# A gated delta rule on Trainium2: the triangular inverse of its chunks formed from 64x64 products in quarters of the PE array

## The chip, the core and the metric

One NeuronCore of a Trainium2 chip runs the whole program. Its engines work side by side and wait for each other by semaphores: TensorE (PE in the profile, its weight loads PEld), VectorE (DVE), ScalarE (ACT), GpSimd (POOL) and SyncE (SP), which issues most of the DMAs. The metric is the device time of one execution in microseconds (us), lower is better.

## What is computed

The reference is a trunk of two layers over 1024 tokens of width 1024. The first layer mixes tokens with a gated delta rule (4 heads) beside stick-breaking attention (8 heads), the second with multi-scale retention; a SwiGLU FFN follows each. The change touches only the delta rule:

```python
def gated_delta_rule(q, k, v, g, beta):            # GDN_CHUNK = 64
    ...
    g = lax.cumsum(g.reshape(b_, h, n, c), axis=3)
    dec_strict = jnp.exp(jnp.where(strict, gdiff, -jnp.inf))
    kb = k * beta[..., None]
    lower = jnp.einsum('bhnid,bhnjd->bhnij', kb, k) * dec_strict
    tri = jnp.eye(c, dtype=lower.dtype) + lower
    rhs = jnp.concatenate([v * beta[..., None], kb * jnp.exp(g)[..., None]], axis=-1)
    sol = lax.linalg.triangular_solve(tri, rhs, left_side=True, lower=True, unit_diagonal=True)
    ...
    def step(state, inp):
        u_n, w_n, a_n, q_n, k_n, gl_n = inp
        v_new = u_n - jnp.einsum('bhcd,bhde->bhce', w_n, state)
        o_n = jnp.einsum('bhcd,bhde->bhce', q_n, state) + jnp.einsum('bhij,bhje->bhie', a_n, v_new)
        state = state * jnp.exp(gl_n)[..., None, None] + jnp.einsum('bhcd,bhce->bhde', k_n, v_new)
        return state, o_n
```

Per head and chunk a unit lower triangular matrix is solved against a right-hand side. The kernel works in chunks of 128 tokens and forms the inverse of that matrix (transposed) outright.

## The kernel before

The program runs through stages: the adaLN modulation and the first norm, the hybrid projection with the delta rule woven into it, stick-breaking attention, the first layer's output and FFN, retention, and the second FFN. Nearly all of its time goes to matmuls of the projections, done in three passes on high and low parts (`mm3`, lines 159 to 161, 128x512 each, tiles named `gps`, `fps`, `ops`).

The change lies in the stage that the profile shows from about 100 to 602 us. There, the remaining projection work (generators `gemm_gen`, tile `gps`; `v_gen`, tile `vps`; the q/k norms, tile `qst`) is the filling between the steps of the delta rule. One step of filling is one k-slice of a projection tile, three 128x512 matmuls.

The delta rule is cut into 8 units, `g_unit(h, b)`, one for each head h and half b of the tokens. A unit handles four chunks of 128 tokens side by side: a tile of 128x512 holds four 128x128 matrices. It is a generator, and each `yield` ends a step. Its steps are: decays (`gd`, `egr`), the norms of k and q (`gst`), the transpose of v (`vT`), `kk` (the products of k with itself, from which DVE makes the upper triangular `U2`), `kT` and `qk`, then the inverse, then the recurrence over the four chunks (`seq`), and the output norm.

The inverse is built by block doubling. Masks (`gc[:, 2 + l]`) cut level l of U2 into `Ul` on POOL. Level 0 gives `Y = I - U0`. Each of the levels 1 to 6 then takes three steps: the PE transposes Y into `X`; the PE forms `W` from Ul and X; the PE forms `dY` from W and Y, and DVE subtracts it from Y. Between them X is copied out of PSUM by ACT or DVE in turn, and W by ACT:

```python
            for l in range(1, 7):
                for c in range(4): PE.transpose(cc(ps, c), cc(Y, c), ident)                      # L742
                (A.copy if l % 2 else V.tensor_copy)(X, ps)                                      # L745
                for c in range(4): PE.matmul(cc(ps, c), cc(u, c), cc(X, c), ...)                 # L749
                A.copy(W, ps)                                                                    # L752
                for c in range(4): PE.matmul(cc(ps, c), cc(W, c), cc(Y, c), ...)                 # L756
                V.tensor_tensor(Y, Y, ps, op=ALU.subtract)                                       # L758
```

An fp32 matmul leaves two records in the profile, a transpose one; a step of four 128x128 matmuls is a row of eight records, and a step of four transposes a row of four.

The order of the PE's instructions is written out by the program (`manual_schedule` over the PE alone); the other engines' order is made by the scheduler, in which the copies of the inverse have a raised priority. The loop at the end of the stage keeps up to three units alive; a new one starts when the youngest has gone `GSTAG` = 14 steps. Each round lets every live unit do one step, and after each step issues a number of filling steps: a credit made of `GFILL` (by how many units live), a weight `GW` for the kind of step, and the filling that is left over the steps that are left. `GSTEPS` says how many steps a unit is counted for.

Of the kernel before, what the change touches and what calls it, by code (L numbers as in the profile page):

```python
# [52 lines left out]
C_ID, C_ONE, C_STRICT, C_INCL, C_NSTR, C_NCOM, C_NEG, C_BLK, C_LEV = 0, 1, 2, 3, 4, 5, 6, 7, 8  # L53
# [8 lines left out]
def tile_trunk(ctx: ExitStack, tc: tile.TileContext, xT, cT, adaS, adaT, vec, w_ab, w_hyb, w_hout, w_rin, w_rout,  # L62
               w_fin, w_fout, cst, rcst, out):
    nc = tc.nc
    V, A, G, PE = nc.vector, nc.scalar, nc.gpsimd, nc.tensor
# [19 lines left out]
    ident, ones = cs[:, 0, :], cs[:, 1, :]  # L85
# [491 lines left out]
    with tc.manual_schedule(engines=PEONLY):  # L577
# [29 lines left out]
        for k in range(8):  # L607
# [22 lines left out]
    with ExitStack() as sx:  # L630
        gq = sx.enter_context(tc.tile_pool(name="gdn", bufs=2, side="right"))
        pb = sx.enter_context(tc.tile_pool(name="pb", bufs=4, space=PSUM))
        gc = gq.tile([P, 9, P], F32, tag="gc", name="gc", bufs=1)
        nc.sync.dma_start(gc[:, 0:2, :], cst[:, C_STRICT:C_INCL + 1, :])
        nc.sync.dma_start(gc[:, 2:9, :], cst[:, C_LEV:C_LEV + 7, :])
# [4 lines left out]
        def bc(ap):  # L640
            return ap.unsqueeze(1).broadcast_to([P, 4, P])
# [4 lines left out]
        r4 = lambda t: t.rearrange("p (c n) -> p c n", c=4)  # L646
        bank = lambda nm: pb.tile([P, HT], F32, tag="b", name=nm)
# [9 lines left out]
        def g_unit(h, b):  # L657
            sl = slice(b * HT, b * HT + HT)
            cs = slice(4 * b, 4 * b + 4)
            tl = lambda tag, bufs: gq.tile([P, HT], F32, tag=tag, name=f"{tag}{h}{b}", bufs=GB.get(tag, bufs))  # L660
            io = []
            for j in range(3):
                t = tl("kn", 3) if j == 1 else tl("gin", 4)
# [9 lines left out]
            ps = bank("gd")  # L673
# [7 lines left out]
            ps = bank("egr")  # L681
# [19 lines left out]
            cc = lambda t, c: t[:, c * P:c * P + P]  # L701
            ps = bank("vT")
# [9 lines left out]
            V.tensor_tensor(U2, ps, Eb, op=ALU.mult)  # L712
            ul = []

            def level(l):
                t = tl("Ul", 3)
                G.tensor_tensor(r4(t), r4(U2), bc(gc[:, 2 + l, :]), op=ALU.mult)
                return t
            u0, u1 = level(0), level(1)
            Y = tl("Y", 2)  # L720
            V.tensor_tensor(r4(Y), bc(ident), r4(u0), op=ALU.subtract)
            yield
            ps = bank("kT")
            for c in range(4):
# [4 lines left out]
            ps = bank("qk")  # L729
            for c in range(4):  # L730
                PE.matmul(cc(ps, c), cc(k, c), cc(q, c), start=(c == 0), stop=True, skip_group_check=True)
            AT = tl("AT", 3)
            V.tensor_tensor(AT, ps, Em, op=ALU.mult)
            yield
            un = u1
            for l in range(1, 7):
                u = un
                if l < 6:
                    un = level(l + 1)
                ps = bank("X")  # L740
                for c in range(4):
                    PE.transpose(cc(ps, c), cc(Y, c), ident)  # L742
                X = tl("X", 1)
                with tc.high_priority(offset=3000):
                    (A.copy if l % 2 else V.tensor_copy)(X, ps)  # L745
                yield "X"
                ps = bank("W")
                for c in range(4):
                    PE.matmul(cc(ps, c), cc(u, c), cc(X, c), start=(c == 0), stop=True, skip_group_check=True)  # L749
                W = tl("W", 2)  # L750
                with tc.high_priority(offset=3000):
                    A.copy(W, ps)  # L752
                yield "W"
                ps = bank("dY")
                for c in range(4):
                    PE.matmul(cc(ps, c), cc(W, c), cc(Y, c), start=(c == 0), stop=True, skip_group_check=True)  # L756
                with tc.high_priority(offset=3000):
                    V.tensor_tensor(Y, Y, ps, op=ALU.subtract)  # L758
                yield "Y"
# [81 lines left out]
        with tc.manual_schedule(engines=PEONLY):  # L841
            gg_ = [gemm_gen(hs, g_evac(i)) for i in range(2, 16)]
            fills = gg_ + [v_gen(0, lambda: gst.tile([P, HT], F32, tag="gy", name="gyv", bufs=2))] + qk_gens
            fill(fills, 8)
            decays()
            heads = {h: gg_[max(4 * h - 2, 0):4 * h + 2] for h in range(4)}
            sizes = {id(g): 32 if i == 14 else 16 for i, g in enumerate(fills)}
            left = 8 * GSTEPS

            def ngroups():  # L850
                return sum(sizes[id(g)] for g in fills) - 8
            units = [(h, b) for h in range(4) for b in range(2)]
            live = []
            credit = 0.0
            acb = []
            aq = [(i, ch, dt) for i in range(2) for ch in (2, 4, 3, 5) for dt in range(8)]

            def ada_half():
                if not aq:
                    return  # L860
                i, ch, dt = aq.pop(0)
                if (ch, dt) == (2, 0):
                    acb.append(gq.tile([P, HT], F32, tag="acb", name="acb", bufs=1))
                    nc.sync.dma_start(acb[i], cb_d[:, i * HT:i * HT + HT])
                w = half_tile()
                j = ch * 8 + dt
                nc.sync.dma_start(w, adaT[j][:, i * HT:i * HT + HT])
                V.scalar_tensor_tensor(w, w, 1.0, acb[i], op0=ALU.mult, op1=ALU.mult,
                                       accum_out=(mod, mod2)[i][:, j:j + 1])
                if i and dt == 7:  # L870
                    ada_finish(0, ch)
            while units or live:
                while units and len(live) < 3 and (not live or live[-1][1] >= GSTAG):
                    h, b = units.pop(0)
                    while any(g in fills for g in heads[h]):
                        fill(fills, 1)
                    live.append([g_unit(h, b), 0])
                for u in list(live):
                    try:
                        hint = next(u[0])  # L880
                        u[1] += 1
                    except StopIteration:
                        live.remove(u)
                        continue
                    left -= 1
                    if left % 4 == 0:
                        ada_half()
                    credit += GFILL[len(live)] * GW.get(hint, 1.0) * ngroups() / max(left, 1)
                    fill(fills, int(credit))
                    credit -= int(credit)  # L890
                    if len(fills) <= SFIRST and not scrs:
                        s_first()
            fill(fills, 999)
            if not scrs:
                s_first()
            while aq:
                ada_half()
# [8 lines left out]
    with ExitStack() as sx:  # L906
# [99 lines left out]
        with tc.manual_schedule(engines=COMPUTE):  # L1006
# [17 lines left out]
            fills = [v_gen(1, stage3)]  # L1024
# [8 lines left out]
            for n in range(-6, 88):  # L1033
                p, m = n // 20, n % 20
# [25 lines left out]
                for tok in SORDER:  # L1060
# [6 lines left out]
                    else:  # L1067
                        i = n + int(tok[1:])
# [471 lines left out]
    o, fpa = ret["o"], ret["fpa"]  # L1540
# [362 lines left out]
```

## Time and profile before

| | |
|---|---|
| device time, median of 3 runs | 3121.37 us (3117.11 to 3124.62) |
| the profiled execution: its time, its span | 3122.01 us, 3120.1 us |
| the clock granted to TensorE, mean | 0.994 |
| PE, DVE, ACT, POOL busy, share of the span | 96%, 68%, 40%, 15% |
| the stage of the delta rule, first to last filling step | about 100 to 602 us |
| records of the inverse on the PE (L742, L749, L756) | 192, 384, 384 |

How to read it: a group row of the profile names the line, the engine, the operation, what it writes and reads, the shape and the count, then its busy time, the mean length of one in ns, and the idle time of its engine just ahead of it with what ended that. A timeline row begins with its start and its length in us; rows that follow each other in the same group are merged (x8). The PE is pipelined: a record lasts longer than the distance to the next one, so what an instruction costs the PE is read from start to start.

### The profile page before, as it was taken

The numbers are of one execution on the slowest core, as the hardware profiler recorded it, in microseconds if no ns is written. First come the engines' busy times: TensorE is split into PE (matmuls) and PEld (weight loads), VectorE is DVE, ScalarE is ACT, GpSimd is POOL, SyncE is SP. The second block draws the span as 40 slices with busy tenths as digits, with TensorE's granted clock in tenths as the row PEclk, the third lists the DMA queues.
The fourth block names the chain that finished last, engine by engine and source line by source line (L and its number), as shares of the span: only waits on it lengthen the run. The fifth ranks groups of instructions, "written<-read, shape, count | busy, mean of one in ns | idle before, by whom it ended". The sixth has DMA issues, their size and how long they took to land. (4 is left out here: it accounts for less than half of the span.)

```text
span 3120.1 us, 38627 instructions
## 1 busy us (share of the span) xinstructions
PE 3004.1 (96%) x14616; PEld 2415.6 (77%) x14616; DVE 2117.9 (68%) x3065; ACT 1244.7 (40%) x2011; POOL 461.7 (15%) x332
## 2 busy tenths in 40 slices
PE   7989999999989999999999999999999899999999
PEld 4778788867667888877878788887777688887887
DVE  6778976599887655588582455578866975556445
ACT  5445456688763222221263333333233632223111
POOL 0333332177440000000030000001111300000000
PEclk9999999999999999999999999999999999999999
DMA  5433332331034322287124333362312352225222
GB/s 215 135 102 122 116 111 73 105 132 45 28 112 149 105 81 81 100 307 260 61 92 152 116 118 111 108 234 92 109 48 70 123 155 85 81 81 167 91 74 101
DMA packets 136602, 362.35 MB, mean 116 GB/s; under 512 B 15072, under 2 KB 24032, under 8 KB 135904
## 3 DMA queue, kind: packets, MB, share of 16 engines
q1 hardware_dynamic: 135808, 358.90, 34.4%
q8 instruction: 115, 1.88, 0.2%
q10 hardware_dynamic: 464, 0.79, 0.1%
q14 instruction: 71, 0.58, 0.1%
q0 software_dynamic: 144, 0.20, 0.0%
HBM read 282.76 MB, written 77.07 MB: 115 GB/s over the span
## 5 line engine op out<-in xcount | busy, mean ns | idle before, releaser
L307 DVE SCALAR_TENSOR_TENSOR x<-ops,mod,x 128x512 f32<-128x512 f32 x288 | 215.3, 749 | 217.9 <-PE ops L161 217.4
L139 ACT CAST whi<-raw 128x1024 fp32r<-128x1024 f32 x158 | 165.5, 1051 | 401.2 <-PE ops L160 305.8
L159 PE MATMUL ops<-hdh,whi 128*128 128x512 f32 x704 | 277.3, 394 | 9.0 <-DVE x L307 8.5
L140 DVE TENSOR_TENSOR wlo<-raw,whi 128x1024 fp32r<-128x1024 f32 x158 | 208.2, 1319 | 104.6 <-ACT whi L139 99.8
L160 PE MATMUL ops<-hdl,whi 128*128 128x512 f32 x704 | 275.7, 392 | 0.0
L161 PE MATMUL ops<-hdh,wlo 128*128 128x512 f32 x704 | 275.5, 391 | 0.0
L159 PEld LDWEIGHTS ops<-hdh,whi 128*128 128x128 f32 x704 | 133.0, 189 | 43.9 <-DVE x L307 14.0
L159 PE MATMUL gps<-hh,whi 128*128 128x512 f32 x352 | 166.1, 472 | 0.0
L161 PEld LDWEIGHTS ops<-hdh,wlo 128*128 128x128 f32 x704 | 132.7, 189 | 28.4 <-issue 0.2
L160 PEld LDWEIGHTS ops<-hdl,whi 128*128 128x128 f32 x704 | 133.0, 189 | 27.3 <-issue 0.2
L195 POOL TENSOR_TENSOR nscr<-nscr 128x512 f32<-128x512 f32 x30 | 46.2, 1541 | 692.7 <-ACT nscr L194 635.0
L1269 ACT CAST thi<-raw 128x512 fp32r<-128x512 f32 x180 | 101.8, 618 | 112.0 <-DVE raw L1265 66.7
L160 PE MATMUL gps<-hl,whi 128*128 128x512 f32 x352 | 140.6, 400 | 0.0
L161 PE MATMUL gps<-hh,wlo 128*128 128x512 f32 x352 | 139.5, 396 | 0.0
L956 POOL TENSOR_TENSOR sl<-ab,sh 128x512 fp32r<-128x512 f32 (+1 forms) x80 | 116.2, 1453 | 140.7 <-ACT ab L940 73.8
L159 PE MATMUL ops<-osh,whi 128*128 128x512 f32 x320 | 127.1, 402 | 10.1 <-DVE x L307 8.1
L160 PE MATMUL ops<-osl,whi 128*128 128x512 f32 x320 | 126.6, 397 | 5.0 <-DVE osl L1757 4.5
L161 PE MATMUL ops<-osh,wlo 128*128 128x512 f32 x320 | 125.0, 392 | 0.0
L1270 DVE TENSOR_TENSOR tlo<-raw,thi 128x512 fp32r<-128x512 f32 x180 | 119.2, 709 | 3.3 <-ACT thi L1269 3.3
L1408 ACT ACTIVATE u<-u 128x512 f32<-128x512 f32 x44 | 27.8, 633 | 231.5 <-DVE u L1339 231.5
L1339 DVE TENSOR_TENSOR u<-u,mE 128x512 f32<-128x512 f32 x60 | 41.2, 687 | 112.5 <-PE mE L1279 112.5
L1319 DVE TENSOR_TENSOR u<-u,mB 128x512 f32<-128x512 f32 x60 | 41.2, 687 | 111.4 <-issue 100.1
(425 smaller groups left out, 8434.8 us busy)
## 6 DMA issues: line engine op xcount, KB each, us to landing
raw<-in_w_fin_dram SPq DMA_DIRECT2D x102, 512.0 KB, 3.8
raw<-in_w_rin_dram SPq DMA_DIRECT2D x64, 512.0 KB, 3.9
raw<-in_w_fout_dram SPq DMA_DIRECT2D x52, 512.0 KB, 3.6
adaw<-in_adaT_dram SPq DMA_DIRECT2D x48, 512.0 KB, 4.8
oraw<-hid_d SPq DMA_DIRECT2D x44, 512.0 KB, 6.1
gth<-in_adaT_dram SPq DMA_DIRECT2D x64, 256.0 KB, 3.0
raw<-in_w_hyb_dram SPq DMA_DIRECT2D x28, 512.0 KB, 3.7
hid_d<-c SPq DMA_DIRECT2D x44, 256.0 KB, 2.0
```

The source lines that it names most:

```text
L139: A.copy(hi, raw)
L140: V.tensor_tensor(lo, raw, hi.bitcast(F32), op=ALU.subtract)
L159: PE.matmul(ps, whi, xh, start=start, stop=False)
L160: PE.matmul(ps, whi, xl, start=False, stop=False)
L161: PE.matmul(ps, wlo, xh, start=False, stop=stop)
L195: (V if k > 5 else G).tensor_tensor(acc, acc, sq, op=ALU.add)
L307: V.scalar_tensor_tensor(xs[dt][:, sl], ps, gts(dt), xs[dt][:, sl], op0=ALU.mult, op1=ALU.add)
L956: G.tensor_tensor(s["sl"], s["ab"], s["sh"].bitcast(F32), op=ALU.subtract)
L1269: A.copy(hi, t)
L1270: e.tensor_tensor(lo, t, f32(hi), op=ALU.subtract)
L1319: V.tensor_tensor(s["u2"], s["u2"], s["S2"], op=ALU.add)
L1339: V.tensor_tensor(s["u3"], s["u3"], s["E"], op=ALU.add)
```

## The change

The four 128x128 matrices of a unit are each seen as 2x2 blocks of 64. Levels 0 to 5 fill only the two diagonal blocks, so these levels now work on the diagonal blocks alone: `Ud` (two POOL copies out of U2), `Ul` and the masks `gl` are 128x256 where they were 128x512, with chunk c's upper block on partitions 0 to 63 and its lower block on 64 to 127. A product of a level is eight 64x64x64 matmuls (`prod`, four chunks by two blocks), the upper ones in one quarter of the PE array (rows and columns 0 to 63), the lower ones in another (rows and columns 64 to 127).

The inverse Y and its transpose X are kept side by side in one tile `YX`. X is made once (`X0`, matmuls with the identity). Each of the levels 1 to 5 then has two steps: W from Ul and X, copied by ACT; and `dYX`, two products into one bank, which DVE subtracts from Y and X in one instruction. In level 5 DVE writes the result into a full 128x512 tile Y. Level 6, the block that couples the halves, is two steps of four 64x64 matmuls, each in one quarter (`W6`, `Y6`), with a copy on ACT and one on DVE.

A unit has 13 steps from X0 to Y6 where the six levels had 18. They yield "t"; such units are put at the end of a round, and only the last of a round is followed by filling. `GSTEPS` goes from 42.5 to 37.5. The masks arrive by four DMAs in pieces instead of one.

```diff
-GSTEPS = 42.5
+GSTEPS = 37.5
...
+        for o in (slice(0, 64), slice(64, P)):
+            nc.sync.dma_start(gl[o, 0:6, :], cst[o, C_LEV:C_LEV + 6, o])
+            nc.sync.dma_start(gl[o, 6, :], cst[o, C_ID, o])
...
+            Ud = t64("Ud", 2)
+            for o in halves:
+                G.tensor_copy(Ud[o], r4(U2)[o, :, o])
             def level(l):
-                t = tl("Ul", 3)
-                G.tensor_tensor(r4(t), r4(U2), bc(gc[:, 2 + l, :]), op=ALU.mult)
+                t = t64("Ul", 2)
+                G.tensor_tensor(t, Ud, b64(l), op=ALU.mult)
                 return t
+            def prod(ps, a, x, c0=0):
+                for c in range(4):
+                    for o in halves:
+                        PE.matmul(ps[o, (c0 + c) * 64:(c0 + c) * 64 + 64], a[o, c, :], x[o, c, :],
+                                  start=(c0 + c == 0), stop=True, skip_group_check=True)
-            Y = tl("Y", 2)
-            V.tensor_tensor(r4(Y), bc(ident), r4(u0), op=ALU.subtract)
+            YX = gq.tile([P, 2, 4, 64], F32, tag="YX", name=f"YX{h}{b}", bufs=2)
+            Yt, Xt = YX[:, 0], YX[:, 1]
+            V.tensor_tensor(Yt, b64(6), u0, op=ALU.subtract)
...
+            ps = bank("X0")
+            for c in range(4):
+                for o in halves:
+                    PE.matmul(ps[o, c * 64:c * 64 + 64], Yt[o, c, :], gl[o, 6, :], ...)
+                A.copy(Xt.rearrange("p c n -> p (c n)"), ps[:, 0:256])
+            yield "t"
+            for l in range(1, 6):
+                ps = bank("W")
+                prod(ps, u, Xt)
+                    A.copy(W.rearrange("p c n -> p (c n)"), ps[:, 0:256])
+                yield "t"
+                ps = bank("dYX")
+                prod(ps, W, Yt)
+                prod(ps, Yt, W, 4)
+                    if l < 5:
+                        V.tensor_tensor(YX..., YX..., ps, op=ALU.subtract)
+                    else:
+                        V.tensor_tensor(Xt, Xt, ps[:, 256:]..., op=ALU.subtract)
+                        for o in halves:
+                            V.tensor_tensor(r4(Y)[o, :, o], Yt[o], ps[o, 0:256]..., op=ALU.subtract)
+                yield "t"
+            ps = bank("W6")
+            for c in range(4):
+                PE.matmul(ps[hi, c * 64:c * 64 + 64], r4(U2)[lo, c, hi], Xt[lo, c, :], ...)
+                A.activation(W[hi]..., ps[hi, 0:256], AF.Copy, scale=-1.0)
+            yield "t"
+            ps = bank("Y6")
+            for c in range(4):
+                PE.matmul(ps[lo, c * 64:c * 64 + 64], W[hi, c, :], r4(Y)[hi, c, hi], ...)
+                V.tensor_copy(r4(Y)[lo, :, hi], ps[lo, 0:256]...)
...
-                for u in list(live):
+                turn = sorted(live, key=lambda u: id(u) in tiled)
+                for u in turn:
+                    whole = id(u) not in tiled
+                    tiled.discard(id(u))
...
+                    if hint == "t":
+                        tiled.add(id(u))
...
-                    fill(fills, int(credit))
-                    credit -= int(credit)
+                    if whole or u is turn[-1]:
+                        fill(fills, int(credit))
+                        credit -= int(credit)
```

How the change stands in the PE's order is seen at two places. The first is level 1 of the first unit, which is alone at that time. Before, from W to dY (`x4` counts the matmuls of a step, `gps` is the filling):

```order
L749 MATMUL W<-X_1027,Ul_965 128x128 x4
L159 MATMUL gps<-hh_149,whi 128x512
L160 MATMUL gps<-hl_150,whi 128x512
L161 MATMUL gps<-hh_149,wlo 128x512
L159 MATMUL gps<-hh_151,whi 128x512
L160 MATMUL gps<-hl_152,whi 128x512
L161 MATMUL gps<-hh_151,wlo 128x512
L756 MATMUL dY<-Y_967,W_1043 128x128 x4
```

The same place with the change:

```order
L733 MATMUL W<-YX_980,Ul_978 64x64 x8
L159 MATMUL gps<-hh_151,whi 128x512
L160 MATMUL gps<-hl_152,whi 128x512
L161 MATMUL gps<-hh_151,wlo 128x512
L159 MATMUL gps<-hh_153,whi 128x512
L160 MATMUL gps<-hl_154,whi 128x512
L161 MATMUL gps<-hh_153,wlo 128x512
L159 MATMUL gps<-hh_139,whi 128x512
L160 MATMUL gps<-hl_140,whi 128x512
L161 MATMUL gps<-hh_139,wlo 128x512
L733 MATMUL dYX<-YX_980,W_1061 64x64 x8
L733 MATMUL dYX<-W_1061,YX_980 64x64 x8
```

The step W is eight small matmuls, dYX two times eight, and three filling steps stand between them here instead of two.

The second place is the end of the first unit's inverse, while the second unit is at `kk`, `kT` and `qk`. Before:

```order
L742 MATMUL X<-cs,Y_967 128x128 x4
L159 MATMUL gps<-hh_141,whi 128x512
L160 MATMUL gps<-hl_142,whi 128x512
L161 MATMUL gps<-hh_141,wlo 128x512
L725 MATMUL kT<-cs,kn_1132 128x128 x4
```

With the change:

```order
L786 MATMUL W_1451<-YX_980,U_971 64x64 x4
L159 MATMUL gps<-hh_141,whi 128x512
L160 MATMUL gps<-hl_142,whi 128x512
L161 MATMUL gps<-hh_141,wlo 128x512
L742 MATMUL kT<-cs,kn_1157 128x128 x4
L159 MATMUL gps<-hh_143,whi 128x512
L160 MATMUL gps<-hl_144,whi 128x512
L161 MATMUL gps<-hh_143,wlo 128x512
L793 MATMUL Y_1474<-Y_1043,W_1456 64x64 x4
```

The small steps alternate with full 128x128 steps of the other unit and with filling. Over the whole order the 64x64 matmuls stand in 104 separate places (13 steps by 8 units); at each, the instruction ahead and the one behind use the full array. The steps of the delta rule stand in 246 places between filling, where it was 270.

More of the change, by code (lines that the diff above doesn't have):

```diff
@@ L733, in g_unit @@
             V.tensor_tensor(AT, ps, Em, op=ALU.mult)
-            yield
[L735 to L759, printed above, removed]
+            yield "t"
@@ new lines, in g_unit @@
+            ps = bank("X0")
+            for c in range(4):
+                for o in halves:
+                    PE.matmul(ps[o, c * 64:c * 64 + 64], Yt[o, c, :], gl[o, 6, :], start=(c == 0), stop=True, skip_group_check=True)
+            with tc.high_priority(offset=3000):
+                A.copy(Xt.rearrange("p c n -> p (c n)"), ps[:, 0:256])
+            Y = tl("Y", 2)
+            un = u1
+            yield "t"
+            for l in range(1, 6):
+                u = un
+                if l < 5:
+                    un = level(l + 1)
+                ps = bank("W")
+                prod(ps, u, Xt)
+                W = t64("W", 2)
+                with tc.high_priority(offset=3000):
+                    A.copy(W.rearrange("p c n -> p (c n)"), ps[:, 0:256])
[3 more added lines that the diff above has]
+                prod(ps, Yt, W, 4)
+                with tc.high_priority(offset=3000):
+                    if l < 5:
+                        V.tensor_tensor(YX.rearrange("p i c n -> p (i c n)"), YX.rearrange("p i c n -> p (i c n)"), ps, op=ALU.subtract)
+                    else:
+                        V.tensor_tensor(Xt, Xt, ps[:, 256:].rearrange("p (c n) -> p c n", c=4), op=ALU.subtract)
+                        for o in halves:
+                            V.tensor_tensor(r4(Y)[o, :, o], Yt[o], ps[o, 0:256].rearrange("p (c n) -> p c n", c=4), op=ALU.subtract)
+                G.memset(r4(Y)[64:P, :, 0:64], 0.0) if l == 1 else None
+                yield "t"
@@ new lines, in g_unit @@
+            lo, hi = halves
+            ps = bank("W6")
+            for c in range(4):
+                PE.matmul(ps[hi, c * 64:c * 64 + 64], r4(U2)[lo, c, hi], Xt[lo, c, :], start=(c == 0), stop=True, skip_group_check=True)
+            W = t64("W", 2)
+            with tc.high_priority(offset=3000):
+                A.activation(W[hi].rearrange("p c n -> p (c n)"), ps[hi, 0:256], AF.Copy, scale=-1.0)
+            yield "t"
+            ps = bank("Y6")
+            for c in range(4):
+                PE.matmul(ps[lo, c * 64:c * 64 + 64], W[hi, c, :], r4(Y)[hi, c, hi], start=(c == 0), stop=True, skip_group_check=True)
@@ L871, in ada_half @@
                     ada_finish(0, ch)
+            tiled = set()
             while units or live:
```

12 lines of the change are left out of this document (8 added, 4 removed).

## The prediction

> **What bounds the kernel now.** I read the windows first, to see which engine sets the length of the stage that changes (columns: window, its length, busy us and records of each engine, granted clock, DMA share, GB/s), then PE's waits in it (total us, times, longest), then its groups.
>
> ```profile
> 100.00:602.00 502.00, 468.91 (x2830) 394.26 (x2829) 376.18 (x622) 264.00 (x482) 143.01 (x117) 1.00 0.32 102
> ```
> ```profile
> PE X L742 <- DVE Y L758: 9.3, 8, 3.1
> PE qk L731 <- DVE gin L698: 4.1, 1, 4.1
> PE gst L695 <- ACT gt L692: 4.1, 5, 1.2
> PE X L742 <- DVE kd L727: 3.2, 2, 2.0
> PE W L749 <- DVE X L745: 3.0, 4, 1.8
> PE X L742 <- ACT oT L792: 2.8, 1, 2.8
> PE kT L725 <- ACT vt L706: 2.0, 2, 1.7
> PE X L742 <- DVE Y L721: 1.1, 1, 1.1
> ```
> ```profile
> L749 PE MATMUL W<-X,Ul 128*128 128x128 f32 x384 | 50.9, 275 | 3.0 <-DVE X L745 3.0
> L756 PE MATMUL dY<-Y,W 128*128 128x128 f32 x384 | 50.5, 274 | 0.0
> L742 PE MATMUL X<-cs,Y 128*128 128x128 f32 x192 | 29.7, 277 | 16.3 <-DVE Y L758 9.3 <-DVE kd L727 3.2 <-ACT oT L792 2.8
> ```
>
> PE is busy for 468.9 of the 502 us, DVE for 376.2. The 33.1 us in which PE is not busy are these waits; the rows shown hold 29.6 of them. So the stage lasts as long as PE's instructions and its waits. What shortens another engine counts only through the waits, and each us that PE's own stream gains or loses moves the end. The inverse's share of the waits is 9.3 + 3.2 + 3.0 + 2.8 + 1.1 = 19.4 us. Filling stands in fixed number behind every step, so nothing else can fill in.
>
> **What is removed from PE.** The price of a record is its distance to the next. Timeline rows (start, length):
>
> ```profile
> 307.09 1.06 PE L749 MATMUL W<-X,Ul 128*128 128x128 f32 x8
> 315.00 0.60 PE L742 MATMUL X<-cs,Y 128*128 128x128 f32 x4
> ```
>
> Eight W records take 1.06 us, the last of them 0.275 long (the mean above): (1.06 - 0.275) / 7 = 0.112 us each. Four transposes: (0.60 - 0.277) / 3 = 0.108. Removed are 768 x 0.112 + 192 x 0.108 = 86.0 + 20.7 = **106.7 us**.
>
> **What the 64x64 records cost.** No row shows a 64x64 matmul. The nearest are matmuls on a part of the array's columns, in the attention (`av`, two groups of 64 columns) and the modulation (`apg`, four of 32):
>
> ```profile
> 660.64 0.28 PE L926 MATMUL z<-q,kh 128*128 128x256 f32 x1
> 660.76 0.28 PE L927 MATMUL z<-q,kl 128*128 128x256 f32 x1
> 660.97 0.65 PE L989 MATMUL av<-ls,vt 128*64 128x256 f32 x4
> 661.55 0.38 PE L967 MATMUL Pb<-sh,scr 128*128 128x256 f32 x1
> 661.77 0.28 PE L968 MATMUL Pb<-sl,scr 128*128 128x256 f32 x1
> ```
> ```profile
> 50.42 0.40 PE L160 MATMUL fps<-hl,whi 128*128 128x512 f32 x1
> 50.65 0.39 PE L161 MATMUL fps<-hh,wlo 128*128 128x512 f32 x1
> 50.97 1.07 PE L404 MATMUL apg<-adaw,sc 128*32 128x256 f32 x16
> 51.97 0.50 PE L159 MATMUL fps<-hh,whi 128*128 128x512 f32 x1
> 52.31 0.40 PE L160 MATMUL fps<-hl,whi 128*128 128x512 f32 x1
> ```
>
> Sixteen records of 256 columns took 1.00 us to the next instruction; at twice 0.112 each, one after another, they would take 3.6. So groups run side by side: four records deep for apg, two deep for av. With r the price of a 256-column record and s a remainder, 4r + s = 1.00 and 2r + s = 0.58, so r = 0.21 and s = 0.16. That is 0.82 ns a column; 128 columns cost 0.105, and the measured 0.112 leaves 0.007 a record. For 64 columns I take 0.058, between half of 0.112 and 0.0525 + 0.007.
>
> Per unit, with upper and lower quarter side by side: X0 8 records deep, five W 8 each, five dYX 16 each, W6 and Y6 8 each (one quarter only): 144. Eight units: 1152 x 0.058 = **66.8 us**. Bounds: 1152 x 0.0525 = 60.5 if only the columns count; 129.0 at 0.112 if the halving brings nothing. I stay near the low end, because the weight loads shrink with the columns and run under the stream:
>
> ```profile
> 660.96 0.20 PEld L989 LDWEIGHTS av<-ls,vt 128*64 128x64 f32 x4
> ```
>
> All four loads are over 0.20 us after the first started, within the first pair's 0.21 us of streaming.
>
> The Trainium skill speaks against this ("TensorE: Matmul & The Clock Gate", Part 3): a weight load overlaps matmuls in flight only where their row groups differ. By it each record would pay its load as well. The av row contradicts it: all four loads use all rows, and the second pair lies under the first pair's stream.
>
> **What changing between full array and quarters costs.** Ahead of av the next full record was due at 660.76 + 0.12 = 660.88, and av starts at 660.97: 0.09. Ahead of apg: 50.65 + 0.23 = 50.88 to 50.97: 0.09. Then s = 0.16 (first load and emptying of the array). Behind it the first full record holds PE for 0.22 instead of 0.12 (av) and 0.34 instead of 0.23 (apg): 0.10, its own load laid bare. Sum 0.35. Before, a product followed the filling without any of this. By the order with the change there are 104 such places and none is shared by two units: the pairing of units is written in the loop, but 14 steps of stagger leave one unit at a time in its 13 small steps. 104 x 0.35 = **36.4 us**. Bounds: 0.16 each (16.6) where PE waits for data anyway and entry and exit cost nothing; 0.45 each (46.8) with one more bare load of 0.10 for the change of rows, which no row shows.
>
> PE's own sum: 66.8 + 36.4 - 106.7 = **-3.5 us**.
>
> **Waits.** Per unit 18 dependent steps become 13; one kind of wait (W on DVE's copy of X, 3.0) has no successor in levels 1 to 5. The new ones are W on DVE's YX, dYX on ACT's W, and at the end Y6 on ACT and `seq` on DVE's Y; queued behind each on PE are the filling and the other units' steps, and their evacuations wait in turn. At the old rate, 19.4 / 144 steps = 0.135 us, 104 steps keep 14.0: -5.4. The filling per step grows by 270 / 246 = 1.10, and the other engines get lighter:
>
> ```profile
> L758 DVE TENSOR_TENSOR Y<-Y,dY 128x512 f32<-128x512 f32 x48 | 32.7, 681 | 10.6 <-PE dY L756 10.4
> L745 DVE COPY X<-X 128x512 f32<-128x512 f32 x24 | 16.5, 686 | 9.4 <-PE W L749 6.1 <-PE X L742 3.3
> L752 ACT COPY W<-W 128x512 f32<-128x512 f32 x48 | 27.9, 581 | 44.4 <-PE W L749 44.2
> L745 ACT COPY X<-X 128x512 f32<-128x512 f32 x24 | 14.0, 584 | 19.6 <-PE X L742 19.6
> L717 POOL TENSOR_TENSOR Ul<-U,gc 128x512 f32<-128x512 f32 x56 | 85.0, 1521 | 136.6 <-PE W L749 102.9 <-DVE U L712 21.2 <-DVE Y L721 11.8
> ```
> ```profile
> L971 DVE TENSOR_TENSOR ls<-ls,Pb 128x256 f32<-128x256 f32 x16 | 6.6, 414 | 0.7 <-PE Pb L968 0.5
> L991 ACT COPY ob<-av 128x256 f32<-128x256 f32 x16 | 5.7, 357 | 0.3 <-PE av L989 0.2
> L956 POOL TENSOR_TENSOR sl<-ab,sh 128x256 fp32r<-128x256 f32 x16 | 16.2, 1014 | 92.8 <-ACT ab L940 73.8 <-DVE sh L953 15.3 <-PE ops L161 3.4
> ```
>
> DVE loses 32.7 + 16.5 and gains 32 x 0.681 + 32 x 0.414 = 35.0 (four short ones per unit at the end): -14. ACT loses 41.9 and gains 56 x 0.357 = 20.0. POOL loses 85.0 and gains at most 48 x 1.014 + 16 copies at that price = 64.9. All of it is covered by PE now, so it counts as shorter waits only: I take **-8 us**, and for the bounds -19.4 (all gone) and +4 (the first unit's wait of qk on DVE, 4.1, again as long, should the two extra copies on POOL delay U0). The masks' four DMAs pass SP ahead of the first unit's inputs once, long before the first level: nothing.
>
> **Sum.** 3122.0 (the profiled execution's time) - 3.5 - 8 = 3110.5. The median shown is 0.6 below that execution: 3109.9, rounded to **3110 us**. About 0.2% (6 us) is what a measurement can tell from no change.
>
> **Rivals.**
> - The quarters run one after another (slower). Upper and lower products use different rows and write one bank of PSUM; if the array serves them in turn, X0, W and dYX are twice as deep: 8 x 128 = 1024 more records x 0.058 = +59.4. From 11.5 / 1024 = 0.011 us lost a record it eats the gain. For it: no row has matmuls on a part of the rows. Against it: av's two halves write one bank side by side, on different partitions, as these do. 3169 us.
>
> The Trainium skill has a rule for this ("TensorEngine Tiling (Array Packing)", Restrictions and Gotchas): different row tiles cannot access the same PSUM bank simultaneously. By that rule this rival would hold; no run here shows it, and av differs only in its columns.
>
> - The change of mode is dearer with rows than with columns alone: at 0.55 a place +20.8, 3131 us; it decides from 0.35 + 11.5 / 104 = 0.46. For it: 104 places with two-sided drains. Against it: av and apg, with different groupings, give the same 0.35.
> - The waits stay. DVE is at 75% and PE waits for it wherever its queue happens to stand; eight times 9.3 us is chance as much as length. Then only -3.5 is left: 3118 us, no change.
> - Loads are not hidden in a quarter: 1152 x 0.053 = +61, 3171 us. The PEld row speaks against it.
>
> **How the numbers follow.** Forecast 0.52 (own range 3098 to 3117), waits stay 0.16, dearer mode change 0.14, serial quarters 0.14, bare loads 0.04. Faster by over 0.2% (below 3115): the forecast without its upper end, 0.48. Slower: serial, loads and most of the dearer change, 0.28. The same: the rest, 0.24. The range 3098 to 3140 takes in the forecast, the staying waits and the dearer change; the two cases near 3170 (0.18) are left out.
>
> **What would show it.** The forecast holds if the start-to-start price in an 8-matmul row is 0.46 us plus 0.35, a dYX row about 1.28 to the next full record, the stage near 490 us, and waits of W on DVE's YX that sum to a few us. It fails at the quarters if a W row lasts 0.9 or more in itself, at the mode change if the filling behind it starts later than 0.26 after the stream's end, at the waits if their sum in the stage is still 30.

## The result, and the profile after

| | before | with the change |
|---|---|---|
| device time, median | 3120.85 us (3117.11 to 3124.62, 4 runs) | 3100.23 us (3091.66 to 3102.97, 4 runs) |
| ratio | | 0.9921 (95% interval 0.9906 to 0.9936) |
| profiled execution: time, span | 3122.01, 3120.1 us | 3099.14, 3097.3 us |

Timed once more, beside the experiments e9 to e11, the change had 3094.55 us against 3123.26 (ratio 0.9904, 0.9891 to 0.9918). It is faster by 0.8 to 1.0%; the forecast was 0.35%.

The whole of it arises in the stage of the delta rule. Where that stage ends is read from the first matmul of the attention (`z`), in the view of that tile: count, shortest/median/longest length in ns, first and last start.

```profile
L926 PE MATMUL z<-q,kh x160: 220/280/357, 609.2 to 831.2; 128*128 128x256 f32 x128, 128*128 128x128 f32 x32
```
```profile
L970 PE MATMUL z<-q,kh x160: 220/281/358, 584.3 to 806.5; 128*128 128x256 f32 x128, 128*128 128x128 f32 x32
```

The first row is before, the second the change: 24.9 us earlier, of which 22.8 are left at the end of the span. The same stage in the windows, up to that matmul (columns as in the prediction), before and with the change:

```profile
100.00:609.00 509.00, 475.91 (x2882) 400.69 (x2881) 379.81 (x627) 268.44 (x489) 143.01 (x117) 1.00 0.32 103
```
```profile
100.00:584.00 484.00, 468.28 (x4094) 367.88 (x4094) 337.75 (x619) 250.38 (x472) 111.56 (x131) 0.99 0.34 109
```

PE is idle for 15.7 us where it was 33.1. DVE, which was forecast to lose 14 us, is busy for 42 us less; POOL lost 31 (forecast 20). PE's waits with the change, all of them:

```profile
PE gst L838 <- ACT gt L835: 5.3, 5, 3.4
PE W L733 <- DVE YX L776: 2.7, 3, 1.3
PE qk L748 <- DVE gin L702: 2.6, 1, 2.6
PE seq L811 <- DVE Y L795: 1.8, 3, 0.9
PE gst L699 <- ACT gt L696: 1.6, 1, 1.6
PE seq L804 <- DVE S L827: 1.1, 1, 1.1
PE qst L508 <- ACT gsq L504: 0.6, 1, 0.6
```

Of the inverse's 19.4 us of waits, 2.7 + 1.8 = 4.5 are left. How the new products run on PE, in the timeline of the change:

```profile
303.53 0.39 PE L160 MATMUL gps<-hl,whi 128*128 128x512 f32 x1
303.76 0.40 PE L161 MATMUL gps<-hh,wlo 128*128 128x512 f32 x1
304.09 0.68 PE L733 MATMUL dYX<-YX,W 64*64 64x64 f32 x16
304.60 0.63 PE L733 MATMUL dYX<-W,YX 64*64 64x64 f32 x16
305.17 0.51 PE L159 MATMUL gps<-hh,whi 128*128 128x512 f32 x1
305.51 0.39 PE L160 MATMUL gps<-hl,whi 128*128 128x512 f32 x1
...
307.87 0.68 PE L733 MATMUL W<-YX,Ul 64*64 64x64 f32 x16
308.48 0.50 PE L159 MATMUL gps<-hh,whi 128*128 128x512 f32 x1
```

The product was due at 303.76 + 0.23 = 303.99 and starts 0.10 later. Its first 16 records hold PE for 0.51 us, of which 0.05 go to the first load (the first pair takes that much longer than the others), so 0.46 for 16 records: two at a time, 0.058 for each pair. The second 16 take 0.57, that is 0.46 and 0.10 to empty the array; the filling behind holds PE for 0.34 instead of 0.23. W: 308.48 - 307.87 = 0.61 = 0.46 + 0.15. So a place costs 0.10 + 0.15 + 0.11 = 0.36 and a record pair 0.058: PE's stream is 104 x 0.36 + 1152 x 0.058 = 104.3 us against 106.7 before, -2.4.

The account of the 24.9 us: stream -2.4, waits -17.4. Most of the remaining 5 can be estimated from the traces. One filling step of 0.8 us that came behind 100 us before the change now comes ahead of it. And a wait costs PE more than its idle time. A wait in the timeline before shows it:

```profile
303.39 0.40 PE L161 MATMUL gps<-hh,wlo 128*128 128x512 f32 x1
304.10 0.66 PE L742 MATMUL X<-cs,Y 128*128 128x128 f32 x4 [0.31 <-DVE Y L758]
```

The transposes were due at 303.39 + 0.23 = 303.62, but L161 counts as busy to 303.79, so 0.17 us of the wait are counted as busy time; and the row of transposes lasts 0.66 us where one without a wait lasted 0.60. That is some 0.2 us for each wait. The views of the waits count 30 of them before and 15 now, so about 3 us. Another 1 us stays open.

Why did DVE lose 42 us? Before the change, DVE's instructions were long where POOL ran beside them. First POOL, then DVE in the same stretch of the timeline before:

```profile
126.75 1.44 POOL L699 TENSOR_TENSOR qd<-qd,gin 128x512 f32<-128x512 f32 x1 [1.84 <-DVE gin L698]
```
```profile
125.39 0.68 DVE L868 SCALAR_TENSOR_TENSOR gth<-gth,acb 128x512 f32<-128x512 f32 x1
...
126.99 1.75 DVE L868 SCALAR_TENSOR_TENSOR gth<-gth,acb 128x512 f32<-128x512 f32 x1
```

The same instruction takes 0.68 us when no POOL instruction runs beside it, and 1.75 when it starts under a POOL multiplication that runs to 128.19. Its group, before and with the change, with the subtraction that reads PSUM beside it:

```profile
L868 DVE SCALAR_TENSOR_TENSOR gth<-gth,acb 128x512 f32<-128x512 f32 x64 | 62.1, 974 | 12.4 <-DMA gth<-in_adaT_dram 10.8 <-DMA acb<-cb_d 1.4
```
```profile
L905 DVE SCALAR_TENSOR_TENSOR gth<-gth,acb 128x512 f32<-128x512 f32 x64 | 45.9, 721 | 6.1 <-DMA gth<-in_adaT_dram 6.0
L776 DVE TENSOR_TENSOR YX<-YX,dYX 128x512 f32<-128x512 f32 x32 | 21.8, 682 | 24.7 <-PE dYX L733 24.7
```

Untouched by the edit, it fell from 974 to 721 ns a piece. By the view of the tile, its shortest and median hardly moved (676 and 692 ns before, 671 and 684 now), while the longest fell from 1786 to 1214: 35 of the 64 ran beside a POOL multiplication or copy before, 21 do now. The subtraction, which has one input in PSUM, kept its length (681 before, 682 now).

Not only instructions with two inputs in SBUF are held up. A `TENSOR_SCALAR` with one SBUF input, whose form usually takes 0.42 us (L174 has a mean of 424 ns over 24), took 1.50 beside POOL in the kernel before, POOL first:

```profile
254.33 1.37 POOL L687 TENSOR_TENSOR ee<-ee,gc 128x512 f32<-128x512 f32 x1 [0.32 <-ACT ee L677]
254.48 1.50 DVE L100 TENSOR_SCALAR gt<-gin 128x512 f32<-128x512 f32 x1
```

Of DVE's 42 us, the instructions that the edit replaced make up 14, as forecast: L758, L745 and L721 (the first Y) had 57.9 us before, and L776, L778, L780, L795 and L738 have 43.6 now. The other 28 come from instructions that the edit does not touch, 16 of them from the group above.

### The profile page after: what moved, and what is told of

The parts are those of the page before. It is cut to its first block, busy times and chain, and to the rows that moved or that the text cites. A ratio compares the mean times of both kernels' runs of the same rounds, so it can differ in the third digit from the quotient of the medians.

```text
span 3097.3 us, 41044 instructions
## 1 busy us (share of the span) xinstructions
PE 3000.7 (97%) x15832; PEld 2386.4 (77%) x15832; DVE 2073.9 (67%) x3057; ACT 1226.8 (40%) x1995; POOL 431.6 (14%) x348
## 5 line engine op out<-in xcount | busy, mean ns | idle before, releaser
L161 PE MATMUL ops<-hdh,wlo 128*128 128x512 f32 x704 | 274.8, 390 | 0.0
L161 PEld LDWEIGHTS ops<-hdh,wlo 128*128 128x128 f32 x704 | 132.5, 188 | 28.2 <-issue 0.2
L161 PE MATMUL gps<-hh,wlo 128*128 128x512 f32 x352 | 140.0, 398 | 0.0
L161 PE MATMUL ops<-osh,wlo 128*128 128x512 f32 x320 | 126.3, 396 | 0.0
```

What stands on the lines that cost most here:

```text
L161: PE.matmul(ps, wlo, xh, start=False, stop=stop)
```

## The experiments

Three theories were tested. **S** (the prediction's): waits follow the number of dependent steps, 13 instead of 18. **F**: they follow the filling per step, which GSTEPS raises. **L**: they fell because POOL and DVE got lighter, above all because POOL no longer lengthens DVE's instructions. The table has each run's median and its ratio to the kernel before as timed beside it, and of its profiled execution the first `z`, the busy us of DVE and POOL in the stage and PE's waits in it; the sections follow.

| run | median us | ratio (95%) | first z | DVE | POOL | waits |
|---|---|---|---|---|---|---|
| before | 3120.9 | 1 | 609.2 | 380 | 143 | 33.1 |
| the change | 3100.2 | 0.9921 (0.9906-0.9936) | 584.3 | 338 | 112 | 15.7 |
| e1_gsteps | 3104.6 | 0.9931 (0.9919-0.9944) | 589.7 | 337 | 110 | 21.0 |
| e2_pool | 3111.8 | 0.9959 (0.9947-0.9972) | 600.1 | 352 | 145 | 27.2 |
| e3_dve | 3102.0 | 0.9928 (0.9915-0.9940) | 589.4 | 357 | 122 | 19.8 |
| e4_joint_full | 3144.1 | 1.0053 (1.0035-1.0072) | 632.6 | 371 | 133 | 31.7 |
| e5_memset | 3097.9 | 0.9923 (0.9909-0.9936) | 583.1 | 337 | 129 | 18.0 |
| e6_three_steps | 3094.9 | 0.9914 (0.9900-0.9928) | 584.4 | 327 | 111 | 14.9 |
| e7_masks_dve | 3093.7 | 0.9914 (0.9899-0.9929) | 578.8 | 346 | 66 | 12.0 |
| e8_masks_dve_act | 3094.8 | 0.9915 (0.9901-0.9928) | 577.5 | 343 | 58 | 13.0 |
| e9_all_load | 3137.6 | 1.0043 (1.0030-1.0055) | 624.8 | 362 | 143 | 41.1 |
| e10_before_two_masks | 3107.2 | 0.9949 (0.9936-0.9963) | 598.1 | 360 | 81 | 22.3 |
| e11_three_masks_dve | 3089.8 | 0.9888 (0.9875-0.9902) | 575.2 | 335 | 67 | 8.6 |
| e12_change | 3094.6 | 0.9904 (0.9891-0.9918) | 583.5 | 337 | 112 | 15.4 |
| e13_all_load_apart | 3130.2 | 1.0026 (1.0015-1.0037) | 620.1 | 369 | 141 | 39.9 |
| e14_three_g13 | 3099.8 | 0.9925 (0.9912-0.9939) | 590.5 | 336 | 67 | 21.6 |
| e15_mask_twice | 3099.0 | 0.9920 (0.9906-0.9934) | 586.8 | 350 | 148 | 19.6 |
| e16_mask_fill | 3094.8 | 0.9905 (0.9891-0.9919) | 582.4 | 338 | 148 | 15.6 |

### The number of steps: e6_three_steps

```diff
             for l in range(1, 6):
+                flip()                    # X from Y, eight 64x64 matmuls with the identity, copy on ACT
+                yield "t"
                 ps = bank("W")
...
                 prod(ps, W, Yt)
-                prod(ps, Yt, W, 4)
```

> 64x64 products in quarters, but X is made anew from Y in each level (three steps a level, 18 a unit, GSTEPS 42.5), Y's update alone on VectorE. The records of the inverse are as many as with the change (1152 deep); 40 more changes between full array and quarters: 40 x 0.34 = 13.6 us. POOL as with the change. Theory S (waits follow the number of dependent steps): waits 15.7 + 8 to 15, time 3122 to 3130 us. Theory L: waits as with the change, 3110 to 3117 us.

The window of the stage and PE's waits:

```profile
100.00:584.00 484.00, 469.00 (x4088) 364.47 (x4087) 326.95 (x602) 268.64 (x525) 111.30 (x131) 0.99 0.34 108
```
```profile
PE dY L733 <- ACT W L772: 4.2, 4, 1.6
PE gst L699 <- ACT gt L696: 3.6, 6, 1.2
PE qk L748 <- DVE gin L702: 2.3, 1, 2.3
```

Eighteen dependent steps a unit, as before the change, and waits of 14.9 us. The time, 3094.9 us, lies below both ranges. S is refuted; e4 below shows the other side of it, 13 steps and waits of 31.7 us. The forecast cost in switches did not come either: with 18 small steps a unit the small phases of two units meet, the pairing in the loop puts them side by side, and PE's order has 116 places instead of 144. DVE is 11 us lighter here than with the change (one 128x256 subtraction a level), which helps it, and e3 prices that at some 2 us of waits; it doesn't turn the finding. Keeping X and Y together is therefore not what made the change fast.

### The filling, POOL and DVE, undone one by one: e1_gsteps, e2_pool, e3_dve

```diff
-GSTEPS = 37.5
+GSTEPS = 42.5
```

> The change with GSTEPS back at 42.5 and nothing else undone. Theory F (the waits fell because each step carries more filling): the filling per step falls to 37.5/42.5 = 0.88, PE's waits in the stage go from 15.7 us back towards 33, time 3110 to 3118 us. Theory S (fewer dependent steps) and theory L (lighter POOL and DVE): waits within 4 us of the change's, time 3096 to 3104 us.

```diff
                 G.tensor_tensor(t, Ud, b64(l), op=ALU.mult)
+                if l in (1, 3, 5):
+                    G.tensor_tensor(more, r4(U2)[:, :, 0:112], bc(strict)[:, :, 0:112], op=ALU.mult)
```

> The change with three more POOL multiplications per unit (128x448, written to a tile that nobody reads): POOL is as busy in the stage as before the change (143 us instead of 112). Theory L: DVE instructions that run beside POOL get longer, DVE's busy time rises by some 15 to 20 us, PE's waits by 8 or more, time 3107 to 3114 us. Theories S and F: PE's waits stay, 3097 to 3104 us.

```diff
+                if l in (1, 3, 5):          # after each level's subtraction, raised priority
+                    V.tensor_tensor(more, r4(U2)[:, :, 0:112], bc(strict)[:, :, 0:112], op=ALU.mult)
```

> The change with three more DVE multiplications per unit (128x448, raised priority, written to a tile that nobody reads), in place of the 24 copies of X that the change took from DVE: DVE +15 us of work in the stage, POOL as in the change. Theory L: PE's waits +6 or more, time 3105 to 3112 us. Theories S and F: 3097 to 3104 us.

F (e1): waits +5.3 us and 3104.6 us, between the two ranges; the ratio of 0.9931 has an interval that overlaps the change's, so it is a few us at most. DVE's load (e3): +19 us of busy time brought +4.1 us of waits and 0.9928; as small, and below what L expected of it. POOL's busy time rose by 10 us there without an instruction more, mostly since its 48 masks took 1095 ns each where they took 948: the holding up goes both ways. POOL (e2): +33 us brought DVE's busy time from 338 to 352, the waits to 27.2 and the ratio to 0.9959, clear of the change's interval. The window of e2_pool:

```profile
100.00:600.00 500.00, 472.69 (x4093) 369.03 (x4092) 352.24 (x620) 249.04 (x470) 144.87 (x155) 0.99 0.33 105
```

PE's instructions are those of the change; POOL alone takes back half of the gain.

### The mirror, in the kernel before: e10_before_two_masks

```diff
-                if l < 6:
-                    un = level(l + 1)
+                un = u1
```

> The mirror of e2_pool: the kernel before, with only the masks of levels 0 and 1 made; levels 2 to 6 use that of level 1 again (so the inverse is another matrix). 40 POOL multiplications of 1.5 us are left out, nothing else. Theory L-port: VectorE's lengths beside POOL go back, its busy time falls by 20 to 35 us, PE's waits from 33 to 18 to 24 us, time 3102 to 3112 us. If POOL mattered only together with the new products: 3118 to 3124 us.

The kernel leaves out the masks of levels 2 to 6, so its result is not the inverse; only its time is read.

```profile
100.00:598.00 498.00, 475.05 (x2881) 401.99 (x2879) 360.10 (x625) 267.56 (x486) 81.49 (x77) 0.99 0.33 105
```

With the old products, the old 18 steps and the old filling, taking 62 us off POOL cuts DVE's busy time by 20 us without taking an instruction from it, PE's waits from 33.1 to 22.3, and the time to 0.9949. L holds on both sides.

### By which way POOL acts: e5_memset, e15_mask_twice, e16_mask_fill

```diff
                 G.tensor_tensor(t, Ud, b64(l), op=ALU.mult)
+                if l in (1, 3, 5):
+                    for z in range(3): G.memset(more, float(z))
```

> The change with POOL kept busy by writes alone: nine fills per unit of a 128x448 tile that nobody reads, in the places where the run e2_pool had three multiplications. Theory L-port (what cost time in e2_pool is that a POOL instruction that reads SBUF holds up VectorE instructions with two SBUF inputs): VectorE's instructions keep their lengths, PE's waits 15 to 19 us, time 3097 to 3104 us. Theory L-queue (POOL's own later work, the decays and masks, came late): waits as in e2_pool, 27 us, time 3107 to 3113 us.

This one tells little: the fills have no input, and POOL ran all 72 of them early, starting at 74.5 to 128.8 us, before nearly all of the places that they were meant for. So the pair was made anew in place, with the mask's own tile, which holds the extra work at its level:

```diff
+                if l > 0: G.tensor_tensor(t, Ud, b64(l), op=ALU.mult)           # e15: reads SBUF
+                for z in range(3 if l > 0 else 0): G.memset(t, float(z))        # e16: only writes
                 G.tensor_tensor(t, Ud, b64(l), op=ALU.mult)
```

> The change with each mask multiplication of levels 1 to 5 done twice on POOL, into the same tile (40 x 0.95 = 38 us more; it reads SBUF). Theory L (POOL's load in the stage lengthens PE's waits), as e2_pool had it: waits 24 to 30 us, ratio 0.995 to 0.998. If e2_pool's loss came from its extra tile or place: waits under 19 us, ratio 0.990 to 0.993.

> The change with three fills of the mask's tile ahead of each mask multiplication of levels 1 to 5 (40 x 3 x 0.29 = 35 us more of POOL, which only writes); the tile ties the fills to their places in the stage, which the fills of e5_memset were not. Theory L-port (a POOL instruction that reads SBUF holds up VectorE instructions with two SBUF inputs): VectorE's lengths as with the change, waits 15 to 20 us, ratio 0.990 to 0.993. Theory L-queue (POOL's later work comes late): as e15_mask_twice, waits 24 to 30 us.

The extra groups and the windows, e15_mask_twice, then e16_mask_fill:

```profile
L728 POOL TENSOR_TENSOR Ul<-Ud,gl 128x256 f32<-128x256 f32 x40 | 38.1, 953 | 91.8 <-PE W L735 91.8
100.00:587.00 487.00, 467.35 (x4084) 366.49 (x4082) 350.21 (x617) 246.93 (x467) 147.84 (x171) 0.99 0.33 107
```
```profile
L728 POOL MEMSET Ul<- 128x256 f32 x120 | 38.3, 323 | 87.5 <-PE W L735 83.4
100.00:582.00 482.00, 466.15 (x4090) 366.14 (x4089) 338.36 (x619) 248.71 (x470) 148.41 (x251) 1.00 0.34 109
```

The same 38 us of POOL: as reads they lengthen DVE by 12 us and the waits to 19.6, as writes nothing (DVE 338, waits 15.6, both as with the change). The intervals of the two ratios overlap, but all four timed runs of e16 (3092.09 to 3096.13) lie below all five of e15 (3096.48 to 3103.17). So 38 us more of POOL's own time cost nothing here unless they are reads, which hold up DVE. The Trainium skill has this rule ("SBUF — State Buffer", Who interferes with whom): a VectorE instruction with two SBUF inputs contends with a GpSimd instruction that reads SBUF, not with one that only writes. The runs agree: 974 against 721 ns for a two-input instruction, 681 and 682 for one whose second input is in PSUM, and nothing for the fills. The `TENSOR_SCALAR` of 1.50 us above has one SBUF input and was held up all the same, so two inputs are not the only case.

The size is not settled. e15 missed what L expected of it: 19.6 us of waits instead of 24 to 30, and a ratio of 0.9920 in the range of its rival, by which e2's extra tile or place counted. e2_pool has the same POOL time as e15_mask_twice and 27.2 us of waits instead of 19.6; its pieces are longer (1.3 us against 0.95), read another tile and come at other places, and which of these counts wasn't tried.

### All undone at once: e9_all_load, e13_all_load_apart

Both have e2's and e3's kinds of extra work and GSTEPS 42.5 together; e13 spreads the extra work over five pieces of 128x224 a unit on each engine.

> The change with all three reliefs undone at once: the POOL multiplications of e2_pool, the VectorE multiplications of e3_dve and GSTEPS 42.5 as in e1_gsteps; the 64x64 products stay. If the three account for the fall of the waits: waits 15.7 + 11.4 + 4.1 + up to 5.1 = 31 to 36 us, and what is left against the kernel before is PE's own stream, 2 to 4 us: 3115 to 3121 us. If the shape of the products itself cut the waits: waits under 27 us, 3104 to 3112 us.

> e9_all_load without its flaw (there the extra VectorE instruction wrote the same buffer as the extra POOL one and waited for it): five POOL and five VectorE multiplications of 128x224 per unit, each into a tile of its own, and GSTEPS 42.5; the 64x64 products stay. If the three reliefs account for the fall of the waits, one by one: waits 28 to 36 us, 3113 to 3121 us. If they do not add up, or the products' shape cut the waits: waits under 26 us, 3102 to 3111 us.

e9 is flawed: its two extra instructions wrote the same buffer, and DVE waited there for POOL.

```profile
L788 DVE TENSOR_TENSOR mored<-U,gc 128x448 f32<-128x448 f32 x24 | 23.2, 967 | 17.2 <-POOL more L730 17.1
```

e13 has no such wait, and it still overshoots: 39.9 us of waits where 28 to 36 was expected, 3130 us, slower than the kernel before. Its extra DVE pieces, by the view of their tile (shortest/median/longest ns), and its window:

```profile
L787 DVE TENSOR_TENSOR mv<-U,gc x40: 375/834/924, 120.3 to 479.0; 128x224 f32<-128x224 f32 x40
100.00:620.00 520.00, 480.11 (x4096) 375.53 (x4095) 369.26 (x660) 252.00 (x472) 140.70 (x171) 0.97 0.32 102
```

A piece that takes 375 ns at its shortest took 834 in the median: placed here, they met POOL most times. So the reliefs do not add up one by one: DVE's extra work cost 4 us of waits while POOL was light (e3), and with POOL and the filling put back as well it is 24 in all. The granted clock in the stage is 0.97 instead of 0.99; how much of the time that is was not tried. Why the sum is more than its parts stays open. What stands: with POOL as busy as before (141 us), DVE nearly so (369) and the old filling, the new products gain nothing.

### The joint update without quarters: e4_joint_full

```diff
-                for c in range(4): PE.transpose(cc(ps, c), cc(Y, c), ident)      # each level
+                for c in range(4): PE.matmul(cc(px, c), cc(Y, c), cc(W, c), ...) # dX, 128x128
+                V.tensor_tensor(X, X, px, op=ALU.subtract)
```

> X and Y updated together without transposes, but with full 128x128 products (no quarters, level 6 included, masks and POOL work as before the change). PE's own sum of the inverse: 8 x (4 x 0.108 + 17 x 8 x 0.112) = 125 us, against 107 before and 104 with the change; no change of mode. If PE's stream plus waits set the stage and the waits fall with the steps (S): 3100 + 21 = 3121 us. Under L (POOL back at full width, DVE with two subtractions a level): waits as before or more, 3132 to 3145 us.

```profile
100.00:633.00 533.00, 501.43 (x3048) 426.19 (x3047) 371.43 (x644) 260.26 (x473) 133.03 (x117) 0.98 0.31 99
```

3144 us with 31.7 us of waits: L's range. By count and price PE's records come to 125 us, 19 more than before the change, and 13 steps a unit did nothing for the waits. The run also bears on a part of the change that no theory names: a step that yields "t" has the weight 1.0 in the filling, where X and Y had 1.4 in `GW`. e4 has these weights and GSTEPS 37.5 too and still waits for 31.7 us, so they alone do not cut the waits. The quarters are what makes the change possible: PE pays no more, while the tiles on POOL, ACT and partly DVE shrink to half.

### Further: e7_masks_dve, e8_masks_dve_act, e11_three_masks_dve, e14_three_g13

e7 moves the mask multiplications to DVE, e8 also the copies into Ud to ACT; e11 is e6 with e7's edit; e14 is e11 with GSTAG 13. e12 is the change itself beside e11.

```diff
-                G.tensor_tensor(t, Ud, b64(l), op=ALU.mult)
+                V.tensor_tensor(t, Ud, b64(l), op=ALU.mult)
```

> The change with the mask multiplications (Ul, 48 of 128x256) moved from POOL to VectorE. Theory L: POOL's 45 us leave the stage, VectorE gets 48 x 0.41 = 20 us of work and is held up less (21 us of extra length now): waits 8 to 14 us, time 3090 to 3098 us. If the plain load of VectorE counts more than POOL's interference: 3102 to 3108 us.

> As e7_masks_dve, and the two copies per unit into Ud on ScalarE instead of POOL: another 9 us off POOL, 16 x 0.36 = 6 us more on ScalarE. Theory L: 1 to 3 us below e7_masks_dve. If POOL's rest does not matter: equal to it.

> e6_three_steps with the mask multiplications on VectorE, as in e7_masks_dve. Theory L: POOL out of the way and VectorE lightest of all; waits 8 to 13 us, time 3086 to 3093 us. If the two reliefs overlap: as e6 and e7, 3092 to 3097 us.

> The change itself once more, beside these runs: 3096 to 3101 us where the kernel before takes 3121; if e6_three_steps and e7_masks_dve (ratio 0.9914 each) are faster than it, its ratio here is 0.992 or more.

> e11_three_masks_dve with the next unit started one step earlier (GSTAG 13): the 64x64 matmuls stand in 112 places instead of 116, 4 x 0.34 = 1.4 us less. If PE's stream is now the bound: 0 to 3 us below e11 (ratio 0.988 to 0.989). If the tighter overlap of units brings waits back: ratio above 0.990.

e7 and e8 have lower waits (12.0, 13.0), but their ratios overlap the change's: a gain of 2 us or so that these runs do not show. e8 is not below e7: the 9 us of copies into Ud on POOL don't matter. e6 and e7 alone are not shown faster than e12. e11 is the best version: 3089.84 us, ratio 0.9888, all four runs (3086.80 to 3092.91) below all four of the change beside it (3093.66 to 3096.27), and 8.6 us of waits:

```profile
100.00:575.00 475.00, 466.11 (x4090) 362.90 (x4090) 334.67 (x651) 268.66 (x525) 66.96 (x83) 1.00 0.34 111
```

e14's one step less of stagger undid it: four places fewer on PE, but 21.6 us of waits and 3099.8 us.

## Why the prediction was right or wrong

The forecast was 3110 us; measured were 3100.2, a gain of 0.79% (by the ratio) instead of 0.35%. The direction and the range held; the size did not.

- **PE's records.** Right. 0.058 us a record and upper and lower quarter side by side were forecast, and 0.46 us per 16 records is what was measured.
- **The change of mode.** Right: 0.36 a place against 0.35, the array's rows adding nothing to what its columns cost. PE's stream was -2.4 against -3.5.
- **Serial quarters.** Did not come. The Trainium skill's rule on row tiles and one PSUM bank ("TensorEngine Tiling (Array Packing)", Restrictions and Gotchas) did not bind these products on the diagonal of the array: they share the bank here and run in pairs, 16 records in 0.46 us.
- **Bare loads.** Did not come either. The sixteen loads of a dYX product lie under its own matmuls:

```profile
304.09 0.54 PEld L733 LDWEIGHTS dYX<-YX,W 64*64 64x64 f32 x16 [0.37 <-issue]
```

  They start with the first matmul at 304.09, and the second product follows at 304.60. The Trainium skill's rule that a load overlaps only matmuls of other row groups ("TensorE: Matmul & The Clock Gate", Part 3) does not hold for these products, as it did not for av.
- **The waits: the step that failed.** Forecast -8 us, measured -17.4, of which 14.9 were the inverse's own. The working scaled the waits by the number of dependent steps ("18 dependent steps become 13", -5.4) and took a little more for the lighter engines, each of whose instructions it priced at its length alone. The first part does not hold: e6 has 18 steps and waits for 14.9 us, e4 has 13 and waits for 31.7. The second put at nothing, without a reason, that POOL's reads hold up DVE. The runs showed this in its place: POOL's reads alone moved the waits by 11 us, put back with the new products (e2) or taken from the old ones (e10), though by only 4 in e15. DVE's instructions of the inverse lost 14 us as forecast, and 28 more went from instructions that the edit does not touch; POOL's reads alone move DVE's busy time by 20 us in e10, 14 in e2 and 12 in e15. The row for it was at hand: a group of 128x512 at a mean of 974 ns on an engine where the same shape takes 681. How the rest of the 17.4 divides between DVE's load and the filling is not settled.
- **The 5 us beside stream and waits.** The sum had no term for what a wait costs beyond its idle time, by the estimate above about 3 us.
- **The waits stay.** They did not. The rival called the waits of X on Y chance as much as length (its row has 9.3 us in eight waits together). In e10, with the old products and less POOL work alone, they were 5.5 us in four, so POOL's part of them was not chance.
- **The filling.** Its share, put within the -8, is 3 us of time or so by e1 and not clear of noise.

## What to carry to other kernels

When one engine's waits bound a stage, price a saving on GpSimd also by what it frees on VectorE: look for groups of one shape with a mean well above their median or usual length, and whether GpSimd reads SBUF beside them. Small matmuls in quarters of the array gain little on the PE where each product stands alone, for entering and leaving cost 0.36 us here, as much as six pairs of records. A count of dependent steps was no measure of the waits here; how long the engine that answers is held up was a better one.

## What was not expected of the hardware

A DVE instruction with two SBUF inputs took 1.75 us instead of 0.68 beside a POOL multiplication that reads SBUF, and one with a single SBUF input 1.50 instead of 0.42. 38 us of POOL multiplications added to the stage made DVE's busy time 12 us longer, 38 us of fills left it as it was. Matmuls in two diagonal quarters that write one PSUM bank ran fully side by side (16 records of 64 columns in 0.46 us), with their weight loads hidden.
